# A hybrid decoder layer on one core: the instruction order now comes from a timeline simulation of the program

## The chip, the cores and the metric

The kernel runs on one NeuronCore of a Trainium2 chip. Five engines work side by side, each through its own instruction stream, strictly in order: TensorE (PE; its weight loads are listed as PEld), VectorE (DVE), ScalarE (ACT), GpSimd (POOL) and SyncE (SP), which here issues all DMAs. An instruction that waits for a semaphore holds up everything behind it on its engine. The metric is the device time of one execution in microseconds (us). Before the change three runs took 1537.07, 1538.51 and 1538.57 us: a median of 1538.51 us.

## The reference

One decoder layer on a sequence of 1024 tokens with 1024 channels, in float32:

```
u = rmsnorm(h);  proj = u @ w_in
q, k, v, r, k, v, w, a, g, gate_a, gate_b = split(proj)
y_attn = sliding_window_attention(q, k, v, sinks) @ w_branch_attn   # window 128, 8 heads
y_rwkv = rwkv7_time_mix(r, k, v, w, a, g) @ w_branch_rwkv           # 8 heads of 64
h = h + (sigmoid(gate_a) * y_attn + sigmoid(gate_b) * y_rwkv) @ w_out
h = h + relu(rmsnorm(h) @ w_ff_in)**2 @ w_ff_out                    # 1024 -> 4096 -> 1024
```

The RWKV part is a recurrence over time: each token's state depends on the one before. The kernel takes 64 tokens at a time (a chunk), for two heads side by side.

## The kernel before, in words

Every large matrix product keeps float32 accuracy by three matmuls of split operands (high and low parts); their 128x512 results are the tiles ps_m (line 156, in mm3, called by proj). The weights of one 128-column block come by DMA (wraw, line 147) and are split on ScalarE (whi) and VectorE (wlo).

Phase 1 (function phase1) holds two kinds of work. The first is the projection of u, 36 column blocks: two LoRA inputs, k, v, four of q, twelve for RWKV, and 16 gates (function gate, whose results go to DRAM as gate_d); all of these are long runs of ps_m matmuls that wait for little. The second is a chain of eight RWKV units (four pairs of heads, two halves of the sequence), numbered 0 to 7, and eight attention blocks. A unit has three parts:

- unit_e (lines 460 to 569): decay, keys and scores. Its score matmuls ps_s give SA and SR on VectorE (line 528). SA goes through DRAM (ln_d, line 541) into the tile LT (line 543), in which 15 pairs of VectorE instructions (lines 565 and 566) invert 16x16 blocks; the result goes through DRAM again (lx_d, XT; lines 567 and 589).
- unit_m (lines 570 to 622): from XT it builds the inverses of 64x64 blocks, with small matmuls ps_g, ps_z, ps_x and VectorE and ScalarE between them.
- unit_c: eight chunk steps, each a closed chain of TensorE and VectorE:

```
PE.matmul pu <- XT, G            # in_order, line 162
V.tensor_copy(out=UV[uc, c, :], in_=pu[uc])                         # line 643
PE.matmul(out=pd, lhsT=BKt[:, c], rhs=UV[:, c], ...)                # line 646
V.scalar_tensor_tensor(out=nxt[hs, hs], in0=pd[hs, hs], ...)  # x2  # sbd, lines 653, 656
PE.matmul(out=ry, lhsT=ARf[:, cp, par], rhs=cur, ...)               # line 636, next step
V.tensor_add(out=Rs[uc], in0=Rs[uc], in1=ry[uc])                    # G, line 638; then pu
```

After the eight steps py, a group norm (a Newton chain of small VectorE instructions, tile nw) and y follow, and y goes to DRAM (yr_d, line 686).

Buffers tie units together: AR, UV, SA, SR and XT have two buffers, G (G0), BK and LT one. So unit_e of unit n+1 is written ahead of unit_c of unit n in the program, and the filling work (gates, attention: strings in PLAN) behind it. unit_e, unit_m and unit_c stand in tc.high_priority blocks (HP_E = HP_C = 3000).

Behind phase 1 its tiles are released, and yh and yl (the split branch outputs; lines 759 to 765) take their place. The branch projections (wbr), the output projection (wout, line 915 for its last part) and the MLP (lines 982 and 1082: 112 blocks of 24 matmuls by a Strassen-like scheme) follow.

Nothing in the kernel fixes the order in which instructions of different chains stand on an engine, but for a few short chains held by in_order. The tile scheduler does it when the TileContext closes: it keeps the dependencies and the buffers, plays the program through on a model of the machine, and takes from what is ready the instruction of the highest priority. The order that comes out is fixed in the program.

## Time and profile before

| | us |
|---|---|
| median of 3 runs | 1538.51 |
| the profiled execution, its time | 1539.05 |
| its span (first to last instruction) | 1537.3 |
| TensorE busy | 1491.2 |
| VectorE busy | 1039.3 |
| ScalarE busy | 638.9 |
| GpSimd busy | 195.3 |

Busy times are of instructions in work; a matmul's end is modelled, so that two that follow each other overlap in the list, and the distance of their starts tells more than their duration. A wait in brackets, as [0.97 <-PE pu L162], is the idle time of the engine ahead of the instruction, and what ended it. The units' chunk steps run from 219.9 to 575.4 us, phase 1's last gate matmul starts at 704.92 us, and the rest of the kernel takes the remaining 832 us.

### The profile page before, as it was taken

Reading aid. Unit: us, or ns where it says so; the run is one execution under the profiler, and the core shown is the slowest. Engines: PE = TensorE matmul, PEld = TensorE weight load, DVE = VectorE, ACT = ScalarE, POOL = GpSimd, SP = SyncE. Lnnn points to the kernel's source line nnn. Section 1 sums busy time; section 2 is a strip of 40 time slices with the busy share of each in tenths; the row PEclk is TensorE's granted clock in tenths of the full one; section 3 lists DMA queues with packets and bytes.
Section 4 is the critical chain, followed back from the end, with each engine's and each line's share of the span. In section 5 each row is a group of like instructions: output and inputs, shape, how many; then the busy total and the mean of one; then the engine's idle time right before and its main releaser. Section 6 shows DMA issues by size and latency. Waiting matters only on the chain.

```text
span 1537.3 us, 22192 instructions
## 1 busy us (share of the span) xinstructions
PE 1491.2 (97%) x8396; PEld 1179.0 (77%) x8396; DVE 1039.3 (68%) x2055; ACT 638.9 (42%) x1126; POOL 195.3 (13%) x117
## 2 busy tenths in 40 slices
PE   5999999999999999999999989999999999999998
PEld 5877767777777777788878777878787878787776
DVE  4232678888989875344656569495968587776767
ACT  6322446556545655532224343242334243424332
POOL 1000000000000000000000112322323232323230
PEclk9999999999999999999999999999999999999999
DMA  5455334334322324372442111112011111111112
GB/s 191 164 154 139 109 117 133 111 97 118 97 83 65 99 97 140 126 268 103 157 152 89 41 41 49 62 41 69 31 66 41 69 42 55 55 54 43 55 55 110
DMA packets 99771, 145.65 MB, mean 95 GB/s; under 512 B 26448, under 2 KB 48848, under 8 KB 99664
## 3 DMA queue, kind: packets, MB, share of 16 engines
q1 hardware_dynamic: 99664, 144.23, 28.6%
q8 instruction: 66, 1.08, 0.3%
q14 instruction: 41, 0.34, 0.1%
HBM read 108.54 MB, written 35.65 MB: 94 GB/s over the span
## 4 chain that ended last, share of the span: by engine, by line
PE 76%; DVE 18%; issue 2%; DMA 2%; ACT 1%; SPq 0%; DVEq 0%; ACTq 0%
PE ps_m L156 31%; PE psy L982 17%; PE psx L982 12%; DVE wlo L924 2%; PE po L156 2%; PE ps_o L915 1%; PE pu L162 1%; DVE h L1082 1%; DVE c L987 1%; DVE tlo L1010 1%; DVE c L1057 1%; DVE c L1015 1%; DVE c L1017 1%; PE pk L238 1%; PE ps_s L162 1%
## 5 line engine op out<-in xcount | busy, mean ns | idle before, releaser
L156 PE MATMUL ps_m<-uh,wlo 128*128 128x512 f32 x576 | 235.4, 409 | 0.0
L156 PE MATMUL ps_m<-ul,whi 128*128 128x512 f32 x576 | 234.3, 407 | 0.0
L156 PE MATMUL ps_m<-uh,whi 128*128 128x512 f32 x576 | 232.9, 404 | 0.0
L982 PE MATMUL psy<-T,whi 128*128 128x512 f32 x512 | 159.6, 393 | 0.0
L156 PEld LDWEIGHTS ps_m<-uh,wlo 128*128 128x128 f32 x576 | 108.6, 189 | 21.2 <-issue 0.6
L156 PEld LDWEIGHTS ps_m<-uh,whi 128*128 128x128 f32 x576 | 108.6, 189 | 21.1 <-issue 0.8
L156 PEld LDWEIGHTS ps_m<-ul,whi 128*128 128x128 f32 x576 | 108.7, 189 | 20.1 <-issue 0.7
L982 PEld LDWEIGHTS psy<-T,whi 128*128 128x128 f32 x512 | 96.1, 188 | 21.6
L982 PE MATMUL psx<-tlo,whi 128*128 128x512 f32 x256 | 101.9, 398 | 7.3 <-DVE tlo L1010 7.3
L982 PE MATMUL psy<-T,wlo 128*128 128x512 f32 x256 | 101.4, 396 | 4.4 <-DVE wlo L924 4.4
L149 DVE TENSOR_TENSOR wlo<-wraw,whi 128x512 fp32r<-128x512 f32 x101 | 67.8, 687 | 55.9 <-ACT whi L148 55.8
L924 DVE TENSOR_TENSOR wlo<-fraw,whi 128x1024 fp32r<-128x1024 f32 x47 | 62.3, 1326 | 62.8 <-ACT whi L923 62.8
L982 PE MATMUL psx<-thi,wlo 128*128 128x512 f32 x256 | 101.1, 396 | 0.9 <-DVE h L1082 0.9
L982 PE MATMUL psx<-thi,whi 128*128 128x512 f32 x256 | 101.1, 395 | 0.0
L1082 DVE TENSOR_TENSOR h<-h,psx 128x1024 f32<-128x1024 f32 (+1 forms) x66 | 78.0, 1183 | 20.3 <-PE psx L982 20.0
L953 POOL TENSOR_TENSOR fraw<-fraw,fraw 128x1024 f32<-128x1024 f32 x16 | 43.0, 2686 | 348.4 <-DVE s L929 347.3
L923 ACT CAST whi<-fraw 128x1024 fp32r<-128x1024 f32 x47 | 49.2, 1046 | 82.3 <-PE psx L982 57.3
L1010 DVE TENSOR_TENSOR tlo<-c,thi 128x1024 fp32r<-128x1024 f32 x56 | 78.2, 1397 | 2.2 <-ACT thi L1009 2.2
L148 ACT CAST whi<-wraw 128x512 fp32r<-128x512 f32 x105 | 61.0, 619 | 44.2 <-PE ps_m L156 44.1
L982 PE MATMUL psy<-thi,wlo 128*128 128x512 f32 x192 | 75.8, 395 | 0.0
L982 PE MATMUL psy<-thi,whi 128*128 128x512 f32 x192 | 75.7, 395 | 0.0
L982 PE MATMUL psy<-tlo,whi 128*128 128x512 f32 x192 | 75.7, 394 | 0.0
(300 smaller groups left out, 3230.5 us busy)
## 6 DMA issues: line engine op xcount, KB each, us to landing
wraw<-win SPq DMA_DIRECT2D x72, 256.0 KB, 3.3
fraw<-wff SPq DMA_DIRECT2D x32, 512.0 KB, 3.2
wraw<-wff SPq DMA_DIRECT2D x32, 512.0 KB, 3.2
gate_d<-gt SPq DMA_DIRECT2D x32, 256.0 KB, 2.0
z_d<-zt SPq DMA_DIRECT2D x24, 256.0 KB, 2.1
xt<-x SPq DMA_DIRECT2D x8, 512.0 KB, 5.7
la<-wa_d SPq DMA_DIRECT2D x8, 512.0 KB, 4.3
aq<-q_d SPq DMA_DIRECT2D x8, 512.0 KB, 4.4
```

The source lines that it names most:

```text
L148: A.copy(out=hi[:, ks], in_=raw[:, ks])
L149: (eng or V).tensor_sub(out=lo[:, ks], in0=raw[:, ks], in1=hi[:, ks].bitcast(F32))
L156: PE.matmul(out=out, lhsT=a, rhs=b, start=(n == 0), stop=(n == last))
L162: after = PE.matmul(out=out, lhsT=lhsT, rhs=rhs, start=start, stop=stop).ins
L238: PE.matmul(out=ps_out[:, col + 2 * i:col + 2 * i + 2], lhsT=sq[:, i * 128:(i + 1) * 128], rhs=c_("ind"), start=True, stop=True)
L915: PE.matmul(out=pss[j], lhsT=a, rhs=b[:, sl], start=(k == 0 and n == 0), stop=(k == NK - 1 and n == 2))
L923: A.copy(out=hi, in_=src)
L924: V.tensor_sub(out=lo, in0=src, in1=hi.bitcast(F32))
L953: G.tensor_sub(out=a21, in0=a11, in1=a21)
L982: PE.matmul(out=out, lhsT=a, rhs=b, start=start and n == 0, stop=n == last, skip_group_check=True)
L1010: V.tensor_sub(out=lo, in0=src, in1=hi.bitcast(F32))
L1082: V.tensor_add(out=ht, in0=ht, in1=ps[:, c0 % 2:c0 % 2 + step])
```

## The change

One argument of the TileContext is added. The scheduler then decides what is ready when by a timeline simulation of the whole program, instead of by its own simple machine model. Instructions, tiles, buffers and priorities stay the same.

```
-    with tile.TileContext(nc) as tc, ExitStack() as ctx:
+    with tile.TileContext(nc, schedule_with_timeline_sim=True) as tc, ExitStack() as ctx:
         hybrid_block(ctx, tc, *aps, out)
```

What it does to the order, at three places. First SyncE, whose stream shows how far the filling work is: around the write of a unit's scores, ln_d_486 being unit 4's and ln_d_487 unit 5's, and gate_d_92 to gate_d_107 the results of the 16 gates. Before:

```order
L541 DMA ln_d_487<-SA 16x8x16 x4
L407 DMA z<-z_d_127 128x512
L750 DMA gate_d_92<-gt 128x512
L541 DMA ln_d_487<-SA 16x8x16 x4
L147 DMA wraw<-win 128x512
```

And now:

```order
L750 DMA gate_d_107<-gt 128x512 x2
L147 DMA wraw<-wbr 128x512 x2
L389 DMA ya_d<-ya 128x2x128
L330 DMA aq<-q_d 128x8x128
L332 DMA ak<-k_d 128x4x256
L409 DMA z<-z_d_124 128x513
L541 DMA ln_d_486<-SA 16x8x16 x8
```

Before, the first gate was stored among the scores of unit 5; now the last of the 16 is stored ahead of the scores of unit 4.

Second TensorE, in the chunk steps of unit 7 before and unit 5 now (pu, pd and ry are a step's matmuls, ps_m the large ones, po, ps_t attention). Before:

```order
L646 MATMUL pd<-UV,BKt 128x128
L156 MATMUL po<-ph,av 128x256
L156 MATMUL ps_m<-uh_141,whi 128x512
L156 MATMUL ps_m<-uh_142,wlo 128x512
L156 MATMUL ps_m<-ul_150,whi 128x512
L636 MATMUL ry<-sbd_478,AR 128x128
L343 MATMUL ps_t<-ak,aq 128x256
```

And now:

```order
L646 MATMUL pd<-UV,BKt 128x128
L636 MATMUL ry<-sbd_479,AR 128x128
L162 MATMUL pu<-G_5283,XT 64x64 x2
L162 MATMUL py<-UV,SR 64x64 x16
L579 MATMUL ps_g<-UV,SA 64x64 x16
```

Before, large matmuls and attention stood between the links of a step; now the links of the later units follow each other directly, and the large ones that stood there have moved ahead of them. Counted over the whole stream, 465 of the 1728 ps_m matmuls of phase 1 stood behind the last of the 64 chunk steps before, and none stands behind the 22nd now; those 1728 are cut into 283 runs before and 117 now.

Third VectorE, at the inverse of unit 6 (LT; two rows are one of its 15 pairs) and the chunk steps of unit 5 (UV, sbd, G). Before:

```order
L643 COPY UV<-pu 64x128
L566 TENSOR_REDUCE LT<-LT 128x5
L135 TENSOR_TENSOR nw<-nw 128x8
L565 TENSOR_TENSOR LT<-LT 128x6x7
L136 SCALAR_TENSOR_TENSOR nw<-nw 128x8
L566 TENSOR_REDUCE LT<-LT 128x6
L137 SCALAR_TENSOR_TENSOR nw<-nw 128x8
L656 SCALAR_TENSOR_TENSOR sbd_478<-pd,wc,sw 64x64 x2
L565 TENSOR_TENSOR LT<-LT 128x7x8
```

And now, the end of the inverse and the first copy behind it:

```order
L482 TENSOR_SCALAR th<-th 128x512
L565 TENSOR_TENSOR LT<-LT 128x8x14
L484 SCALAR_TENSOR_TENSOR cum<-smask,th 128x512
L566 TENSOR_REDUCE LT<-LT 128x8
L565 TENSOR_TENSOR LT<-LT 128x8x15
L566 TENSOR_REDUCE LT<-LT 128x8
L565 TENSOR_TENSOR LT<-LT 128x128
L566 TENSOR_REDUCE LT<-LT 128x8
L130 TENSOR_SCALAR nw<-pk 128x8
L131 TENSOR_SCALAR nw<-nw 128x8
L643 COPY UV<-pu 64x128
```

Before, the pairs of the inverse stood between the links of the chunk steps; now all 15 pairs of this unit's inverse stand ahead of the copy of the next unit's first step (the 41st of 64). For units 4, 5 and 7 most pairs stand so. 101 of the 320 VectorE instructions of attention stand behind the 22nd copy.

## Rows read from the trace of the kernel before

**Rows 1.** The page, busy time of each engine, share of the span, instructions
```profile
PE 1491.2 (97%) x8396; PEld 1179.0 (77%) x8396; DVE 1039.3 (68%) x2055; ACT 638.9 (42%) x1126; POOL 195.3 (13%) x117
```

**Rows 2.** Longest wait of TensorE: for whom, us in total, times, longest
```profile
PE pt L221 <- DVE xt L211: 16.4, 1, 16.4
```

**Rows 3.** Busy us by stage: length, PE, PEld, DVE, ACT, POOL, PEclk, DMA
```profile
219.20:576.00 356.80, 353.07 (x3178) 266.07 (x3178) 306.42 (x1095) 207.58 (x517) 5.88 (x28) 1.00 0.33 102
576.00:705.00 129.00, 128.06 (x629) 102.14 (x626) 53.89 (x143) 59.23 (x138) 0.00 (x0) 1.00 0.49 167
705.00:1537.30 832.30, 809.21 (x3482) 651.33 (x3480) 582.02 (x554) 286.21 (x325) 181.06 (x63) 1.00 0.19 67
```

**Rows 4.** The same of ps_m alone, in the stretch of the eight units
```profile
219.20:576.00 356.80, 188.01 (x596) 100.36 (x594) 0.00 (x0) 14.72 (x25) 1.00 0.33 102
```

**Rows 5.** TensorE by time: start us, us, line, out<-in, count
```profile
103.84 0.98 PE L238 MATMUL pk<-cst,sq 128*128 128x2 f32 x8
104.69 0.48 PE L156 MATMUL ps_m<-ul,whi 128*128 128x512 f32 x1
105.00 0.39 PE L156 MATMUL ps_m<-uh,whi 128*128 128x512 f32 x1
...
704.92 0.39 PE L156 MATMUL ps_m<-uh,whi 128*128 128x512 f32 x1
705.15 0.39 PE L156 MATMUL ps_m<-yh,wlo 128*128 128x512 f32 x1
```

**Rows 6.** All engines, the links of two chunk steps of unit 7
```profile
551.31 0.44 PE L162 MATMUL pu<-G,XT 64*64 64x64 f32 x4
551.79 0.28 DVE L643 COPY UV<-pu 64x128 f32<-64x128 f32 x1 [0.97 <-PE pu L162]
552.25 0.38 PE L646 MATMUL pd<-UV,BKt 128*128 128x128 f32 x2
...
552.67 0.58 DVE L656 SCALAR_TENSOR_TENSOR sbd<-pd,wc,sw 64x64 f32<-64x64 f32 x2 [0.33 <-PE pd L646]
...
556.77 0.40 PE L636 MATMUL ry<-sbd,AR 128*128 128x128 f32 x2
557.20 0.28 DVE L638 TENSOR_TENSOR G<-G,ry 64x128 f32<-64x128 f32 x1
557.55 0.44 PE L162 MATMUL pu<-G,XT 64*64 64x64 f32 x4
```

**Rows 7.** VectorE, from scores to inverse and from inverse to unit_m, unit 7
```profile
501.75 0.42 DVE L528 TENSOR_TENSOR SR<-ps_s,cst 128x256 f32<-128x256 f32 x1
...
510.46 0.16 DVE L565 TENSOR_TENSOR LT<-LT 128x2 f32<-128x2 f32 x1
...
527.45 0.29 DVE L566 TENSOR_REDUCE LT<-LT 128x8 f32<-128x128 f32 x1
...
538.44 0.71 DVE L591 STREAM_TRANSPOSE XD<-XT 128x512 f32<-128x512 f32 x1
```

**Rows 8.** VectorE lines: ns min/median/max, first and last start us, forms
```profile
L643 DVE COPY UV<-pu x64: 255/289/297, 219.9 to 575.4; 64x128 f32<-64x128 f32 x64
L565 DVE TENSOR_TENSOR LT<-LT x120: 141/282/383, 185.3 to 527.1; 128x2 f32<-128x2 f32 x8, 128x6 f32<-128x6 f32 x8, 128x12 f32<-128x12 f32 x8, 128x20 f32<-128x20 f32 x8
L566 DVE TENSOR_REDUCE LT<-LT x120: 130/218/292, 186.6 to 527.5; 128x1 f32<-128x2 f32 x8, 128x2 f32<-128x6 f32 x8, 128x3 f32<-128x12 f32 x8, 128x4 f32<-128x20 f32 x8
```

**Rows 9.** Timeline: last y of phase 1, first yt load, last yl
```profile
586.59 0.69 DVE L685 TENSOR_TENSOR y<-y,bv 128x512 f32<-128x512 f32 x1 [1.12 <-ACT y L683]
...
644.92 1.29 SPq L759 DMA_DIRECT2D yt<-ya_d  x3
...
674.63 1.23 DVE L765 TENSOR_TENSOR yl<-yt,yh 128x1024 fp32r<-128x1024 f32 x1 [1.11 <-ACT yh L764]
```

**Rows 10.** Busy us by stretch, granted clock after the POOL column (PEclk)
```profile
888.00:891.00 3.00, 2.29 (x5) 1.82 (x6) 3.00 (x6) 1.86 (x3) 0.00 (x0) 0.61 0.07 14
```

**Rows 11.** TensorE after its second longest wait
```profile
888.71 7.35 PE L982 MATMUL psy<-B,c 128*128 128x512 f32 x24 [5.32 <-DVE h L886]
```

## The prediction

> **What bounds the kernel now.** I read the engine shares first, then the longest waits of TensorE, then the busy times by stage. TensorE is busy for 97% of the span [rows 1], and its one long wait is the start, 16.4 us [rows 2]. By stage [rows 3] it stays so where the work is of two kinds: from 219.2 to 576 us, the eight RWKV units, TensorE is busy 353.1 of 356.8 us and VectorE 306.4 of them. From 576 to 705 us VectorE has little to do (53.9 of 129.0) and TensorE is still full. So the time now is the sum of TensorE's work, and that holds because large projection matmuls (ps_m) stand between the small matmuls of the RWKV units, whose steps wait for VectorE. Between 219.2 and 576 us there are 596 of them [rows 4], and in the 129 us behind come the projections that are left, gates above all. A new order can win at most the few idle microseconds. It can lose whatever it leaves without large matmuls beside it.
>
> **The change part by part.** No instruction is added or removed; all that changes is their order on each engine.
>
> What moves on TensorE: at the 22nd of the 64 chunk steps (unit_c) the new order has already issued the last of the 1728 ps_m matmuls of the projections and gates; before, 465 were left behind step 64. So 42 chunk steps, five runs of unit_m, four inversions of unit_e (L565, L566) and a third of the attention stand alone at the end of phase 1. I go along TensorE up to the last gate, through that tail, and through the joint to the branch projections (wbr).
>
> *Up to the last gate.* Before, it ends at 705.2 us, where the first matmul on yh starts [rows 5]. The small matmuls that move behind it: in 219.2 to 576 us the 596 large ones take about 596 x 0.25 = 149 us (0.23 start to start within a run [rows 5], more at its end), so 208 us are small work. That stretch holds 64 steps, 7 runs of unit_m, 6 units' score matmuls, and 114 of the 180 po matmuls; 42, 5, 4 and 66 of these move, less what of unit_e still stands earlier. I take 0.55 of 208 us: 115 us (104 to 125). Fewer changes between large and small: the first large matmul after small ones takes 0.31 us to the next instead of 0.23 [rows 5], and the runs of ps_m fall from 283 to 117: 166 x 0.08 = 13 us gained. Stalls on the way: between unit 0's scores and its ps_z the new order has 72 large and some small matmuls, about 25 us. The path there is 2 us on VectorE, 8.3 to the inverse through DRAM, 8.3 for the inverse, about 14 us of attention and other work put between, and 10.7 back through DRAM (527.7 to 538.4) [rows 7]: 43 us, so 18 are lost. The first chunk steps have no large matmuls (about 7 us lost), and at the starts of units 1 and 2 about 38 and 34 us of TensorE work face some 43 on VectorE (about 10). Sum 35 us (10 to 60). Last gate: 705 - 115 - 13 + 35 = 612 us.
>
> *The tail.* One chunk step, read link by link [rows 6]: pu to the UV copy 0.48, copy 0.28, then pd, 0.42 until sbd, sbd 0.58, then ry, 0.43 until the G add, add 0.28, then pu. With the small gaps that is 2.7 us when nothing else is queued. With the present filling the last unit takes (575.4 - 551.8) / 7 = 3.4 us [rows 6, 8]. Before, the inversions stand between the chunk steps. In the new VectorE order all 15 pairs of unit 6's inverse stand ahead of the UV copy of step 41, and most pairs of units 4, 5 and 7 ahead of steps 25, 33 and 49. VectorE goes in order, so these wait for their own DMA first. Queued behind that copy are pd, on TensorE everything behind pd, and all later steps. From the copy of step 40 to that of step 41:
> - 8 wide instructions of about 0.69 us [rows 9], 10 of 0.42 [rows 7], sbd and G 0.87, 14 tiny ones at 0.2: 13.4 us to the last score product;
> - 8.3 us until the inverse can start: 502.2 to 510.5 [rows 7], three small DMA hops;
> - 15 pairs of 0.28 + 0.22 us [rows 8] and 0.05 of gap: 8.3 us, and seven others among them 5 us.
>
> That is 35 us. Seven steps of 2.7 and 5 us of work that they don't hide make the period 59 us. Units 3, 4 and 5: 3 x 59 = 177. Unit 6 has no later unit to begin, 59 - 11 = 48. Unit 7 takes 13.4 for unit_m (538.4 to 551.8 [rows 6, 7]) and 18.9 for steps, 32. The end of unit 2 is 8. The attention left has 101 of its 320 VectorE instructions, at most 0.38 us each (53.9 / 143 [rows 3]); half of that hides in the steps' gaps, 20 us. Sum 285 us.
>
> The clock: after a wait of 5.32 us [rows 11] the granted clock was 0.61 in the next 3 us [rows 10], mostly 1.2 instead of 2.4 GHz, and 24 matmuls took 7.35 us instead of 24 x 0.23 = 5.6. Such waits will come in every period of the tail. I add 10 us: 295 (255 to 335).
>
> The Trainium skill ("TensorE: Matmul & The Clock Gate", section "HAM oscillation — how this bites in real kernels") says that a loop whose idle gaps are long enough falls back to half the clock in every turn. The one wait that the trace has agrees with it; what it would make of the whole tail is the second rival.
>
> *The joint.* yh and yl lie where phase 1's tiles lay, so their loads start when the last unit is done. Before, y ended at 587.3, 11.6 us after the last copy, with attention between [rows 8, 9]; I take 10. From the first yt load to the last yl it took 644.9 to 675.9 = 31 us [rows 9], hidden behind gates that are now gone. One group of 12 matmuls, 3 us, can run in it. 10 + 31 - 3 = 38 us (33 to 42).
>
> *The rest*, 832.3 us [rows 3], keeps its order but for small swaps: 0, plus or minus 8 us. The gate loads and stores go earlier on the SP queue and find TensorE busy beside them, so I count them at nothing; if a weight load sits behind a DMA that waits, that is in the 35 us of stalls.
>
> Sum: 612 + 295 + 38 = 945 us where 705 stood: +240. The profiled execution took 1539.05 us (span 1537.3), 0.5 above the median of the runs. 1539 + 240 = 1779 us.
>
> **The rivals.**
> 1. The tail overlaps as well as the units do now. 64 copies from 219.9 to 575.4 us are 5.64 us a step with all that belongs to it [rows 8]; 42 of them 237 us. 612 + 237 + 38 is +182: 1721 us. For it: VectorE has less other work in the tail (no weight splits, little attention). Against it: the order puts the inverses in front of the steps, and VectorE can't pass them.
> 2. The clock stays at 1.2 GHz through the tail. TensorE's part of a step is 0.48 + 0.42 + 0.43 = 1.33 us [rows 6]; if half of it is streaming that doubles, 42 x 0.67 = 28 us, and about 17 in five runs of unit_m: 45 instead of 10, 1814 us. For it: waits far above 5 us in each period. Against: TensorE never idles long in seven steps of a unit, so it may recover there.
> 3. Not slower: the tail costs no more than TensorE's own 115 us, and the 13 us of fewer changes are won, with 2 to 3 us of short waits: about 1524 us. It decides whether VectorE's unit work disappears in the 1.5 us that a step leaves it free, so that 42 steps x 2.7 = 113 us are all there is. Against it: 42 x 1.5 = 63 us are too little for four inverses, with their DMA hops, and the rest of unit_e.
>
> That the change does nothing is excluded: the order differs on every engine.
>
> **How the numbers follow.** Forecast 1779 us, chance 0.68, its own range 1725 to 1832 from the bounds above (stalls 25, tail 40, joint 5, moved work 10 either way, taken as independent). Rival 1: 0.15. Rival 2: 0.13. Rival 3: 0.03. Something else: 0.01. The range 1705 to 1850 takes in rivals 1 and 2 with their spread. A difference of 0.2%, 3 us, is about what can be told from none. Faster 0.03, same 0.01, slower 0.96.
>
> **What would show it.** In the profile after: TensorE full up to about 610 us, then a stretch of nearly 300 us with TensorE busy for less than half and VectorE busy for about two thirds; waits of pd or pu for VectorE behind L566; of VectorE for the DMA into LT, some 6 us in each of four places; copies of UV at 2.7 us in runs of seven; the first matmul on yh near 930 us and a wait of 25 us or more inside the first branch projection; the last 832 us as before. Wrong would be: a tail under 220 us (then the inverses hide), a last gate beyond 670 us (then the stalls up front are mis-sized), or PE full to the end of phase 1.

## The result and the profile after

The changed kernel takes 1746.9 us (median of four runs, 1743.87 to 1749.61) where the one before takes 1538.36 (four runs, 1537.07 to 1538.57): 208.5 us more, a ratio of 1.1357 with a 95% interval of [1.1335, 1.1379]. The profiled execution took 1749.61 us, its span is 1747.8. The forecast was 1779 us. One run of the version with the gates paced over units 3 to 7, 2510.82 us at a granted clock of 0.55, was in a slower state of the chip and is left out of its median below.

The page of the changed kernel: busy time, share and instructions [rows 1], then three of its rows of 40 slices, 43.7 us each. A digit is a tenth.

```profile
PE 1571.5 (90%) x8396; PEld 1258.5 (72%) x8396; DVE 1054.0 (60%) x2055; ACT 639.6 (37%) x1126; POOL 194.0 (11%) x117
...
PE   5989979999999977665649999999999999999998
...
PEclk9999989999999957656559999999999999999999
DMA  4455234342333221100053341111111111211112
```

The instructions are the same in number, but TensorE is busy 80 us longer than before [rows 1]. What to look at is one hole, slices 15 to 21: there TensorE is less busy, at a lower granted clock, and the DMA row falls to 0 in three of them. A busy engine at half its clock is not doing more work, so the two rows have to be read together.

Stages of the changed kernel, columns as in [rows 3]: up to the last gate, to the last UV copy, unit 7's steps alone, the joint to the last yl, the rest.

```profile
219.20:589.30 370.10, 356.80 (x2271) 287.81 (x2270) 193.97 (x639) 165.91 (x402) 2.51 (x15) 0.97 0.34 110
589.30:878.20 288.90, 199.96 (x1695) 154.62 (x1695) 184.03 (x622) 99.93 (x251) 3.60 (x16) 0.63 0.13 36
851.00:879.00 28.00, 16.93 (x76) 11.55 (x76) 8.28 (x29) 4.23 (x13) 0.00 (x0) 0.50 0.00 1
878.20:923.90 45.70, 18.00 (x74) 12.01 (x75) 22.04 (x34) 10.03 (x11) 0.00 (x0) 0.61 0.53 190
923.90:1747.80 823.90, 803.51 (x3444) 646.65 (x3442) 574.41 (x550) 284.61 (x322) 179.95 (x63) 0.99 0.19 67
```

The same for ps_m alone [rows 4]: all of it lies in front of 589.3 us, none in the tail (one record ends on the bound).

```profile
219.20:589.30 370.10, 263.86 (x1041) 191.10 (x1039) 0.00 (x0) 25.47 (x43) 0.97 0.34 110
589.30:878.20 288.90, 0.04 (x1) 0.00 (x0) 0.00 (x0) 0.60 (x1) 0.63 0.13 36
```

UV copies, minimum, median and maximum in ns, first and last start [rows 8]; then VectorE from the last copy of unit 4 to the first of unit 5 [rows 7].

```profile
L643 DVE COPY UV<-pu x64: 243/288/296, 257.4 to 878.2; 64x128 f32<-64x128 f32 x64
```

```profile
723.13 0.30 DVE L643 COPY UV<-pu 64x128 f32<-64x128 f32 x1
...
735.31 0.41 DVE L528 TENSOR_TENSOR SR<-ps_s,cst 128x256 f32<-128x256 f32 x1
...
742.13 0.16 DVE L565 TENSOR_TENSOR LT<-LT 128x2 f32<-128x2 f32 x1 [4.25 <-POOL LT L544]
...
753.72 0.29 DVE L566 TENSOR_REDUCE LT<-LT 128x8 f32<-128x128 f32 x1
...
754.19 0.28 DVE L643 COPY UV<-pu 64x128 f32<-64x128 f32 x1
```

Between the last copy of unit 4 and the first of unit 5 lie 31.1 us: 12.6 to the end of the score products, 6.4 until the inverse can start, 11.9 for the inverse of unit 6, and the copy comes 0.2 us behind it. The releaser in brackets is the one that came last, a memset on GpSimd that follows the DMA into the same tile; the wait as a whole is the DMA's way through DRAM: SA is written out from 730.3 us, and LT is loaded from 738.4.

TensorE in unit 7, where nothing else is queued [rows 6]:

```profile
854.38 0.69 PE L162 MATMUL pu<-G,XT 64*64 64x64 f32 x4 [0.38 <-DVE G L638]
855.45 0.80 PE L646 MATMUL pd<-UV,BKt 128*128 128x128 f32 x2 [0.39 <-DVE UV L643]
857.08 0.77 PE L636 MATMUL ry<-sbd,AR 128*128 128x128 f32 x2 [0.83 <-DVE sbd L656]
858.22 0.69 PE L162 MATMUL pu<-G,XT 64*64 64x64 f32 x4 [0.37 <-DVE G L638]
```

A step takes 3.84 us (pu to pu), and pd 0.80 us where it took 0.38: the granted clock of the stretch is 0.50, the lower of the two levels, 1.2 GHz. Each wait is under 1 us, and yet the clock stays there for all of the unit.

The joint, all engines [rows 9]:

```profile
889.46 0.69 DVE L685 TENSOR_TENSOR y<-y,bv 128x512 f32<-128x512 f32 x1 [2.33 <-ACT y L683]
...
892.32 1.27 SPq L759 DMA_DIRECT2D yt<-ya_d  x3
...
897.46 0.80 PE L156 MATMUL ps_m<-yh,wlo 128*128 128x512 f32 x1 [9.09 <-ACT yh L764]
...
908.41 0.79 PE L156 MATMUL ps_m<-yh,wlo 128*128 128x512 f32 x1 [5.90 <-ACT yh L764]
```

TensorE idles 27.7 of these 45.7 us, first for the group norm, then for the load and the split of yh and yl.

### The profile page after: what moved, and what is told of

Read it like the earlier page. It is cut to its first block, busy times and chain, and to the rows that moved or that the text cites. A ratio compares the mean times of both kernels' runs of the same rounds, so it can differ in the third digit from the quotient of the medians.

```text
span 1747.8 us, 22162 instructions
## 1 busy us (share of the span) xinstructions
PE 1571.5 (90%) x8396; PEld 1258.5 (72%) x8396; DVE 1054.0 (60%) x2055; ACT 639.6 (37%) x1126; POOL 194.0 (11%) x117
## 4 chain that ended last, share of the span: by engine, by line
PE 35%; DVE 10%; DMA 2%; issue 2%; ACT 1%; SPq 0%; DVEq 0%; ACTq 0%
PE psy L982 16%; PE psx L982 10%; PE ps_m L156 8%; DVE wlo L924 2%; DVE h L1082 2%; PE ps_o L915 1%; DVE tlo L1010 1%; DVE c L1015 1%; DVE c L987 1%; DVE c L1057 1%; DMA yt<-yr_d 1%; DVE c L1017 1%; DVE c L1053 1%; DVE c L1018 1%; ACT c L990 0%
## 5 line engine op out<-in xcount | busy, mean ns | idle before, releaser
L156 PE MATMUL ps_m<-uh,wlo 128*128 128x512 f32 x576 | 231.7, 403 | 1.6 <-DVE wlo L149 1.0
L982 PEld LDWEIGHTS psy<-T,whi 128*128 128x128 f32 x512 | 96.2, 188 | 21.7
L982 PE MATMUL psx<-thi,wlo 128*128 128x512 f32 x256 | 97.2, 395 | 0.0
L982 PE MATMUL psy<-B,whi 128*128 128x512 f32 x240 | 74.8, 393 | 0.0
```

What stands on the lines that cost most here:

```text
L156: PE.matmul(out=out, lhsT=a, rhs=b, start=(n == 0), stop=(n == last))
L982: PE.matmul(out=out, lhsT=a, rhs=b, start=start and n == 0, stop=n == last, skip_group_check=True)
```

## The experiments

Three theories. A, mine: the new order issues all large matmuls early, so that 42 chunk steps are left alone, and the load of yh and yl after them. B: TensorE's half clock in that tail is what costs. C: VectorE's order, the next unit's inverse ahead of the steps, is what costs. Where a kernel queues work behind a link, it does so by an edge of issue order on TensorE or VectorE (tc.issue_after), and no data depends on it. All are compared with the changed kernel's 1746.9 us, and beside each of them the kernel before ran on the same chip (medians of 1538.1 to 1539.3 us). The ratios are to that kernel.

The changes to the kernel are shown shortened. links[n, c] holds the pu and pd of step c (from 0) of unit n; pins is the list of the instructions behind which the next groups of gate matmuls are queued, one entry for each group; fill("x ") writes one gate. All versions but the one named "Inverse behind the steps" also write the last two gates inside phase 1, where the program had them behind the load of yh and yl.

**Warm.**

```
+ for n in range(3, 8):
+     for c in range(8):
+         for a in links[n, c]:            # pu, pd
+             with tc.issue_after(a):
+                 2 x PE.matmul(out=ps_w, lhsT=uh[0][:, 0:128], rhs=uh[0][:, 0:HALF])
```

> The changed kernel plus 158 large matmuls (128x512, two behind every pu and every pd of units 3 to 7, into a PSUM tile that nobody reads) to keep TensorE's clock up while the 42 chunk steps stand alone. In the changed kernel the tail from the last gate (589 us) to the last UV copy (878 us) is 293 us, a plain step is 3.85 us where 2.7 was forecast, and the granted clock is 0.58. Theory A (no large work is left beside the chain of steps, and the clock makes each step longer): the clock comes back in the steps, a step falls to about 2.7 to 3.0 us, 35 steps x 1 us are won: 1705 to 1720 us. Theory B (the half clock is the whole of it: TensorE's work in the tail takes 200 us instead of 115): 1660 to 1670 us. If the clock doesn't matter, the 36 us of added work stand in the way: 1750 to 1785 us.

1725.76 us (ratio 1.1213 [1.1177, 1.1249]): 21 less, with 154 added matmuls, not 158. But the clock came back only in places (0.89 from 620 to 700 us), and not at all in unit 7:

```profile
835.00:864.00 29.00, 26.34 (x88) 17.54 (x87) 7.86 (x28) 4.22 (x13) 0.00 (x0) 0.50 0.00 1
```

TensorE was busy 26.3 of 29.0 us and the granted clock stayed 0.50. So a step grew to 4.2 us there, and the run can't price the clock.

**Warm with six in a row.**

```
- for a in links[n, c]:                    # pu, pd
+ for a in links[n, c][-1:]:               # the last link of the step
-         2 x PE.matmul(ps_w ...)
+         (18 if c == 7 else 6) x PE.matmul(ps_w ...)
```

> The changed kernel with unread large matmuls as before in the warm run, now 6 behind each step's last link and 18 behind the unit's last, in units 3 to 7 (the first try had two behind pu and pd: in the last unit TensorE was busy 26.3 of 29.0 us and the granted clock still 0.50, so that it could not tell what the clock costs). Theory A: at the full clock a step with six of them takes 3.3 us as in the first paced run where it was 3.85 alone at half clock: 35 x 0.5 = 18 us and some 5 us in unit_m: 1720 to 1730 us. Theory B (half clock is the whole of the tail): 1660 to 1670 us. If the clock doesn't come back: 1750 to 1800 us.

1723.53 us (1.1201 [1.1182, 1.1220]), as theory A said. There are 300 added matmuls. From 588.5 to 866 us the granted clock is 0.90, and a step takes 3.3 us with six added matmuls in it. TensorE in unit 7 of this run:

```profile
843.41 0.49 PE L650 MATMUL pd<-UV,BKt 128*128 128x128 f32 x2 [0.37 <-DVE UV L647]
843.66 1.64 PE L752 MATMUL ps_w<-uh 128*128 128x512 f32 x6
845.14 0.38 PE L639 MATMUL ry<-sbd,AR 128*128 128x128 f32 x2
845.90 0.44 PE L162 MATMUL pu<-G,XT 64*64 64x64 f32 x4 [0.38 <-DVE G L641]
846.73 0.49 PE L650 MATMUL pd<-UV,BKt 128*128 128x128 f32 x2 [0.39 <-DVE UV L647]
```

So B falls as the main cause: with the clock back, all but 23 of the 208 us are still there. The 23 are a net figure, since the added matmuls stand in front of ry. Had all of their 300 x 0.23 = 69 us been in the way, the clock would be worth 92 us, still less than half; how much of the 69 was, no run shows.

**Inverse behind the steps.**

```
  V.tensor_copy(out=UV[uc, c, :], in_=pu[uc])
+ with tc.issue_after(cu):                 # that copy, of the unit before
+     inv(range(2 * c + 1, min(2 * c + 3, 16)))      # two of the 15 pairs, units 4 to 7
```

> The changed kernel, but of units 4 to 7 the inverse on VectorE (15 pairs of a product and a sum) is queued two pairs behind each UV copy of the unit before, so VectorE can't wait for the inverse's DMA in front of the chunk steps. Theory C (VectorE's order is what makes the tail long): the 31 us stretches between the first and second step of units 5 and 6 go, each of four units saves 8 to 14 us: 1690 to 1717 us. Theory A (a unit's chain through inverse, DRAM and unit_m has to be walked anyway, and the inverse now ends with the unit's last step): period = 8 steps x 3.9 + 10.7 DRAM + 13.4 unit_m = 55 us against 60, 60, 50, 45 now: 1735 to 1755 us.

1728.16 us (1.1229 [1.1210, 1.1248]): 19 less, between the two theories. The stretch of 31.1 us became 23.2 (710.9 to 734.1), but the other three, in front of units 4, 6 and 7, went from 27.5, 22.7 and 18.3 to 22.7, 24.4 and 21.4 us. The four together are 8 us shorter; the steps of units 3 and 4 give another 8. VectorE of this run, from the last copy of unit 4 over the end of unit 5's inverse to the first copy of unit 5:

```profile
710.89 0.29 DVE L654 COPY UV<-pu 64x128 f32<-64x128 f32 x1
...
712.78 0.28 DVE L570 TENSOR_REDUCE LT<-LT 128x8 f32<-128x128 f32 x1
...
719.72 0.71 DVE L600 STREAM_TRANSPOSE XD<-XT 128x512 f32<-128x512 f32 x1 [0.31 <-issue]
...
734.14 0.28 DVE L654 COPY UV<-pu 64x128 f32<-64x128 f32 x1
```

The inverse now ends 2.2 us behind the last copy, and what is then late is its way through DRAM and unit_m: 6.7 us to XD, 14.4 more to the copy. VectorE's order costs something, but the path that it stood on was nearly as long without it.

**The old scheduler, gates first.** The kernel before, without the change:

```
+ if n == 3:
+     with tc.high_priority(offset=6000):
+         fill("x " * 16)                  # all 16 gates
  unit_c(3): first pu issue_after the last gate matmul
```

> The scheduler of the kernel before, with all 16 gates traced ahead of unit 3's chunk steps and unit 3's first pu queued behind the last gate matmul, so that the steps of units 3 to 7 stand alone as in the changed kernel, but in the old order of VectorE and TensorE (inverse pairs and unit_m between the steps). Theory A (running out of large matmuls is the cause by itself): nearly the same loss, 1690 to 1740 us. Theory C (the timeline order of the small work is a large part): 1600 to 1650 us, since a unit then takes its 45 us (5.64 us a step with all that belongs to it) or less. Unknown is the joint, exposed here as well.

1708.86 us (1.1108 [1.1092, 1.1125]): 170 of the 208 us come without the timeline simulation, by the place of the gates alone. But the place is not quite that of the changed kernel. Almost all gates stand in one run between the first and the second step of unit 2, and the projections of pair 3 go on behind them beside units 2 and 3. First the UV copies of those two steps, then ps_m alone between them and from there to the last of it:

```profile
320.74 0.28 DVE L648 COPY UV<-pu 64x128 f32<-64x128 f32 x1 [0.50 <-PE pu L163]
...
498.61 0.29 DVE L648 COPY UV<-pu 64x128 f32<-64x128 f32 x1 [0.78 <-PE pu L163]
```

```profile
322.00:498.00 176.00, 174.57 (x748) 139.97 (x747) 0.00 (x0) 18.54 (x31) 1.00 0.28 100
498.00:587.50 89.50, 45.34 (x141) 23.34 (x140) 0.00 (x0) 2.94 (x5) 1.00 0.30 94
```

The last large matmul, a projection's, stands in front of step 34 of the 64: 31 steps are left alone here, 42 in the changed kernel. Stages, columns as in [rows 3]: to that matmul, to unit 7's end, attention alone, yh and yl.

```profile
219.20:587.50 368.30, 366.45 (x2475) 282.94 (x2473) 192.09 (x622) 144.68 (x326) 4.35 (x23) 1.00 0.31 104
587.50:765.00 177.50, 139.81 (x1159) 109.70 (x1158) 129.66 (x479) 82.52 (x219) 1.61 (x6) 0.66 0.17 48
765.00:855.00 90.00, 47.23 (x172) 35.72 (x171) 31.74 (x130) 35.27 (x105) 0.00 (x0) 0.52 0.17 53
855.00:878.50 23.50, 12.39 (x23) 6.39 (x24) 14.76 (x13) 8.37 (x8) 0.00 (x0) 0.57 0.90 316
```

The front is full, and here too the clock falls behind the last large matmul. The old scheduler walks the 31 steps in 177.5 us, 5.7 us each, and leaves attention to the end, 90 us; the new order mixes the two. From the last large matmul to the last yl it is 291 us here, with 31 steps in it, and 335 in the changed kernel, with 42. So the run shows that the place of the large matmuls costs by itself, under either scheduler; where the remaining 38 us lie, it can't tell, since the two tails don't hold the same work.

**Three gates for the joint.**

```
- gates 13 to 15 wherever they are ready
+ pins.extend([links[7, 7][-1]] * 24)      # behind the last pu, 6 matmuls each
+ fill("x " * 3)
```

> The changed kernel with 3 of the 16 gates (144 large matmuls, 33 us) queued behind the last pu of unit 7, the other 13 as before. It asks what the joint between phase 1 and the branch projections costs when nothing stands beside the load and split of yh and yl (45 us from the last UV copy to the last yl, 28 of them idle on TensorE). My sum (joint 38 us exposed): the front ends 33 us earlier and the joint becomes no longer: 1713 to 1720 us. Rival: the gates stand in the way of the last y (transposes and py queue behind them) or yh waits for something else, so half is lost: 1728 to 1740 us. If the joint isn't exposed: 1747 us.

1734.36 us (1.1270 [1.1254, 1.1287]): 12.5 less, not 33. The joint was covered (TensorE busy 36.8 of 36.8 us from 857.0 to 893.8), but the last UV copy came only 21.7 us earlier (856.5), because the last steps of unit 2 had lost the gates beside them, and from it to y the way was 19.2 us instead of 11.9, through the gates. The rival was nearer.

**Gates paced over units 3 to 7.**

```
+ for n in range(3, 8):
+     for c in range(8):
+         pins.extend([links[n, c][-1]] * (13 if c == 0 else 1))   # groups of 6
+ pins.extend([links[7, 7][-1]] * 128); del pins[128:]
+ fill("x " * 16)
```

> The same timeline-ordered scheduler, but all 16 gates are kept for the end: in groups of 6 large matmuls, one group queued behind each step's last TensorE link of units 3 to 7, 13 behind the first step of each, and 40 groups behind the last pu, so that 128 groups stand where the changed kernel had nothing. Theory A (the loss is large matmuls spent too early): the front ends 177 us earlier (768 x 0.23), the tail of 293 us takes in 88 groups in its idle time and gets its clock back, the last 40 groups cover the load of yh and yl: 1520 to 1580 us, 1550 likeliest. Theory C (VectorE's order, with the inverses of the next unit ahead of the steps, sets the length, and large matmuls between the links only lengthen the steps): the tail stays near 293 us plus half of the 88 groups (60 us): 1600 to 1650 us.

1689.14 us (1.0975 [1.0957, 1.0993]): 58 less, a miss for A's 1550, and above what C allowed. This version puts 100 groups into the five units and 28 behind the last pu, where 88 and 40 were meant. The main reason is in the stages of this run, first units 1 and 2, then all behind them to the last gate:

```profile
350.00:510.00 160.00, 124.85 (x982) 100.42 (x982) 118.26 (x437) 83.31 (x218) 2.24 (x12) 0.65 0.26 79
510.00:853.00 343.00, 304.82 (x2206) 241.66 (x2206) 185.87 (x578) 123.28 (x286) 2.50 (x11) 0.95 0.26 85
```

The order had spent the other 960 large matmuls by step 9, and the first gate was held for unit 3: the lonely stretch had moved to units 1 and 2, where the clock is now 0.65. And the 13 groups stood in front of the second and third step of each unit (13.7 and 11.5 us behind the one before in unit 6).

**Gates spread in threes from unit 1 on.**

```
+ for n in range(1, 8):
+     for c in range(8):
+         pins.extend([ry, pu, pd of (n, c)])          # 3 matmuls each
+     pins.extend([links[n, 7][-1]] * 8)
+ pins.extend([links[7, 7][-1]] * (256 - len(pins)))
```

> Again the timeline-ordered scheduler with all 16 gates kept back, now from unit 1 on and in threes: 3 large matmuls behind each ry, pu and pd of units 1 to 7, 24 behind each unit's last pd, 96 more behind the last pu. In the first paced run units 1 and 2 had become a new stretch without large matmuls (430 to 510 us: granted clock 0.59, TensorE busy 64 of 80 us) and the groups of 6 stood in front of the links. Theory A (what is lost is only the company of large matmuls): steps of 3.3 us for 56 steps, 22 us from one unit to the next, so 340 us behind the first step of unit 1 at 371 us; joint covered, then 824 us: 1560 to 1600 us. Theory C (the order of VectorE's work, inverse and unit_e ahead of the steps, leaves waits that no filler covers, 10 us and more per unit): 1620 to 1660 us.

1626.84 us (1.0581 [1.0560, 1.0601]): 120 of the 208 us are back, 27 short of A's range, at the low end of C's. (Behind the last pu stand 144 large matmuls, not 96.)

**Spread, and the inverse behind the steps.** Both edits.

> The spread gates together with the inverses of units 4 to 7 queued two pairs behind each copy of the unit before. Theory A: with large matmuls to stand in the holes, the place of the inverse is worth little: within 10 us of the spread run. Theory C: the inverse in front of the first step of a unit still costs its stretch, as where it alone was moved (19 us): 15 to 30 us less than the spread run.

1624.79 us (1.0560 [1.0545, 1.0576]), 2 us from the spread run, whose runs overlap with it. This, and not the time of the spread run alone, is what separates A from C: the inverse's place is worth 19 us where the steps stand alone and nothing that can be told where large matmuls stand beside them.

**Projections paced too.**

```
+ gates on the links of units 0, 2 and 4 to 7 (3 matmuls each, 14 threes behind units 4 to 7)
+ zpins: projections of pairs 2 and 3 on the links of units 1 and 3 (6 matmuls each)
```

> Pacing carried further: besides the gates the projections for pairs 2 and 3 are held back too (6 large matmuls behind each link of units 1 and 3), gates in threes behind the links of units 0, 2 and 4 to 7, 14 threes behind the end of each of units 4 to 7, 72 matmuls more behind the last pu. The count of large matmuls issued by each step is then within some 60 of the kernel before from unit 0 on (774 at step 9, 1062 at step 25, 1350 at step 45). Theory A (what counts is how many large matmuls are left beside the steps, not which scheduler): the 48 us that the spread run had lost by the first step of unit 1 shrink: 1570 to 1600 us. Theory C (waits from the timeline order of the small work): 1615 to 1640 us, as in the spread run.

1607.85 us (1.0451 [1.0436, 1.0467]): 139 of the 208 us back, between the two ranges: 8 us above A's, 7 below C's. Up to the first step of unit 1, from there to y, the joint, the rest:

```profile
219.20:330.00 110.80, 91.97 (x761) 70.93 (x760) 86.44 (x307) 64.89 (x166) 1.69 (x11) 0.86 0.38 120
330.00:753.50 423.50, 401.52 (x3165) 313.09 (x3164) 288.06 (x983) 195.33 (x488) 4.52 (x21) 0.97 0.27 86
753.50:789.10 35.60, 27.35 (x102) 20.02 (x100) 18.52 (x19) 12.12 (x15) 0.00 (x0) 0.90 0.78 295
789.10:1607.00 817.90, 799.04 (x3436) 642.80 (x3436) 569.95 (x550) 284.32 (x322) 180.86 (x63) 1.00 0.19 67
```

In the 423.5 us that hold units 1 to 7 TensorE is busy for 95% at a clock of 0.97. Half of what is still missing, 37 of 69 us, lies ahead of the first step: it comes at 256.8 us against 219.9 [rows 8], behind about as many large matmuls (672 and 669). So there it is not their number; the order of the other work and its waits are left, which no run here takes apart. Nor is the count within 60 of the kernel before later on, as the expectation has it: 774 against 725 large matmuls stand in front of step 9, but 1062 against 913 in front of step 25 and 1536 against 1215 in front of step 57.

**The joint bare again.**

```
- pins.extend([links[n, 7][-1]] * 14)
+ pins.extend([links[n, 7][-1]] * (14 if n < 6 else 52 if n == 6 else 0))
```

> The same, but 114 of the 129 large matmuls (26 us) that stand behind the last pu are queued behind the end of unit 6 instead, so that the joint, 45 us from the last UV copy to the last yl in the changed kernel, has nothing beside it again. My joint term (exposed unless filled): 20 to 30 us more than the run beside it. Rival (the joint isn't what costs there, or unit 7 gains as much as the joint loses): within 8 us of it.

1623.63 us (1.0551 [1.0532, 1.0570]): 16 more, between the two. The 114 matmuls, moved ahead of unit 7, delay its first step by 13 us (722.2 against 709.3) and the last yl by 12 (800.8 against 789.1); the joint is then 48 us from the last copy. It costs, but less than a bare sum says.

No version beat the kernel before.

## Why the prediction was right

The direction held and so did the main mechanism: large matmuls issued early, a long tail of small work behind them and a joint with nothing beside it. The size was 29 us too high: against the profiled execution, 1749.6 where 1779 stood. The clock term was wrong in kind, and the tail came out so close by luck. The terms:

- *Last gate*, 612 forecast, 589.3 measured. TensorE's busy time up to there fell from 682.2 to 550.0 us, 132 us where 115 + 13 = 128 had been forecast, so the moved work and the fewer changes were sized well together (the two can't be told apart, and some of the busy time was at half clock: from 230 to 260 us the granted clock is 0.72). The idle time rose from 23.0 to 39.3 us, by 16 us, where the stalls had been put at 35: that is nearly the whole error.
- *The tail*, 295 forecast, 288.9 measured, by two errors that cancel. The stretch between units was mis-sized at 35 us; the worst, the one that the prediction reckoned, is 31.1: 12.6 + 6.4 + 11.9 where 13.4 + 8.3 + 8.3 + 5 stood. A step was put at 2.7 us and took 3.84. Over units 3 to 7 the stretches sum to 121 us where 142 stood, and the five runs of seven steps to 160 where 94.5 stood, with 50 for other work, attention and the clock beside them. The unit periods, last copy to last copy, are 65.7, 59.9, 60.0, 50.0 and 45.2 us; forecast were 59 three times, 48 and 32, with 20 for attention and 10 for the clock beside them. Unit 7 shows the error unmixed: 18.3 for unit_m where 13.4 stood and 26.8 for seven steps where 18.9 did, 13 us more, without attention and at a clock of 0.50.
- *The clock term*, 10 us, was wrong in kind. The prediction took from [rows 10, 11] that a long wait lowers the clock for a few microseconds, and the second rival was argued down with "TensorE never idles long in seven steps of a unit, so it may recover there". It doesn't: 0.50 through all of unit 7, with waits under 1 us, and 0.63 over the whole tail. By rows, 35 steps x 1.14 us would be 40 us, an estimate, since no run has a step alone at the full clock (2.7 us is put together from links); by the run with six in a row 23 come back, net of what the added matmuls cost. The second rival was right on the clock for the most part, though no wait of TensorE in the tail is above 4.3 us and it had asked for waits far above 5; its 1814 us was too high, as the other terms came out smaller. The Trainium skill ("TensorE: Matmul & The Clock Gate", section "HAM oscillation — how this bites in real kernels") ties the fall to idle gaps above a certain length. The wait of 5.32 us [rows 11] agrees. The tail is not covered by it: there the clock falls at about 615 us, among waits of 0.51, 0.88 and 1.17 us (shown in the last section), and in unit 7 it stays down with none above 1 us.
- *The joint*, 38 forecast from the last copy to the last yl, less the group inside; 45.7 measured. y came 11.9 us after the copy (10 taken), yt to yl took 31.6 (31 taken), and 2.2 us lie between. What matmuls on yh and yl ran in it, some 40, show in the next term; the 3 us taken off for 12 of them should not have stood here. The two runs on it say what it is worth in the time: 12.5 and 16 us, since the matmuls that cover it are missed elsewhere.
- *The rest*, 832 plus or minus 8 forecast, 823.9 measured: some 40 matmuls on yh and yl, 9 us at 0.23, had run inside the joint.

589.3 + 288.9 + 45.7 + 823.9 = 1747.8 us, the span. The forecast's own range is a little wide for its bounds: taken as independent, they give 49 us either way, not 53.

Of the marks named ahead, TensorE full to about 610 us, a stretch of nearly 300 us behind it and VectorE busy for two thirds of it (184 of 289) were there. "TensorE busy for less than half" was not (200 of 289): at half clock the same work is busy for longer. The copies of UV stood 3.84 us apart in unit 7, not 2.7, and the first matmul on yh came at 897.5 us, not near 930. The waits of VectorE for LT are 13.9 us in four places, not 24. No single wait of 25 us stood in the first branch projection: it is split into 9.1, 5.9 and shorter ones.

The first rival, a tail as well overlapped as the units before (5.64 us a step), fails in the changed kernel: 288.9 us for 42 steps. It nearly holds for the units in the old order with the gates first (177.5 us for 31 steps, 5.7 each), but there attention follows alone. The third, not slower, is out.

Why the new order does it is open. It is not the priority of the units: with the two offsets at 100000 instead of 3000 the order on TensorE is the same, instruction by instruction (so it is under the old scheduler), and with both at 0 the small work changes places, but each of the 64 steps has as many large matmuls in front of it as with 3000. This is read from the programs' order alone. That a gate is ready earlier than the next link of a chain is the likely reason, not a shown one.

## What to carry to other kernels

Large independent matmuls beside a chain of short dependent ones are a stock to be rationed: count how many are left at each step of the chain, in the order, before counting anything else. Holding them back by edges of issue order recovered 139 of 208 us, while moving VectorE's work or warming the clock in the empty tail recovered some 20 each; the last 69 us stayed out of reach here. A stock held for one part of the chain is missing in another (units 1 and 2 of the first paced run), so it is spread over all of it and the joint behind it.

## What the runs showed of the hardware

In the tail of the changed kernel the granted clock fell to 0.50 at about 615 us and stayed there for 40 us. No long wait stands in front of that fall, only three short ones. TensorE's matmuls there, and its clock in the four microseconds before and behind 616 us:

```profile
612.69 0.50 PE L162 MATMUL ps_l<-la,lwl 64*128 64x512 f32 x1 [0.51 <-ACT UV L561]
614.06 0.69 PE L617 MATMUL ps_x<-XT,DZ 32*32 32x32 f32 x32 [0.88 <-ACT DZ L613]
615.93 0.58 PE L156 MATMUL po<-ph,av 128*128 128x256 f32 x1 [1.17 <-DVE pl L383]
```

```profile
612.00:616.00 4.00, 1.44 (x46) 0.90 (x38) 1.79 (x12) 3.57 (x9) 0.19 (x2) 0.90 0.32 98
616.00:620.00 4.00, 4.00 (x19) 3.55 (x20) 3.47 (x16) 1.39 (x3) 0.20 (x1) 0.50 0.22 65
```

With two and two large matmuls in each step of unit 7 TensorE was busy for 91% of 29 us, and the granted clock stayed at 0.50; with six in a row in each step it was 0.84 over unit 7, though TensorE was busy for less (81%):

```profile
827.00:853.00 26.00, 21.07 (x102) 16.23 (x103) 7.73 (x28) 4.23 (x13) 0.00 (x0) 0.84 0.00 1
```

At half clock a share of busy time says little, since the work itself takes twice as long (pd 0.80 us against 0.38). And in the joint of the changed kernel the matmuls on yh go from 0.43 us apart to 0.23 at 915.5 us, behind a run of eight without a wait:

```profile
915.10 0.62 PE L156 MATMUL ps_m<-yh,whi 128*128 128x512 f32 x1
915.52 0.44 PE L156 MATMUL ps_m<-yh,wlo 128*128 128x512 f32 x1
915.80 0.40 PE L156 MATMUL ps_m<-yl,whi 128*128 128x512 f32 x1
916.03 0.39 PE L156 MATMUL ps_m<-yh,whi 128*128 128x512 f32 x1
```
